# The tail of the last expert and the output of an encoder block, rearranged

## The chip, the cores and the metric

One core of one Trainium2 chip. The metric is the device time of one execution in microseconds; for several runs it is their median.

## The reference, cut to what matters

One layer of a transformer encoder over 512 tokens of width 1024 in float32: two attentions and a gated output projection, then a mixture of 16 experts in which each expert picks its 64 best tokens, and a last RMSNorm.

```python
def expert_choice_ffn(h, w_router, w_gate, w_up, w_down):
    ...
    gate, idx = lax.top_k(jnp.swapaxes(aff, 1, 2), cap)        # 16 experts x 64 tokens
    xe = h[bidx, idx]
    hid = (jax.nn.silu(jnp.einsum('becd,edf->becf', xe, w_gate))
           * jnp.einsum('becd,edf->becf', xe, w_up))
    ye = jnp.einsum('becf,efd->becd', hid, w_down) * gate[..., None].astype(h.dtype)
    return jnp.zeros_like(h).at[bidx, idx].add(ye)
...
    x = x + gt2 * expert_choice_ffn(h2, ...)                    # gt2: 1024 numbers from the condition
return rmsnorm(x, g_final)
```

Each expert has 2048 hidden columns, so its three weights are 8.4 MB each, 403 MB for all experts.

## The kernel before, in words

The first half of the kernel is the attention part. The second half, from about 915 us on, is the loop over experts (L1170). An expert's weights come in twelve pieces of 2.1 MB (n = 0 to 11): gate and up in turn for n < 8, then w_down in four quarters of 512 rows. `weights` (L1032) takes the next of nine ring slots of 16 KB a partition (`wslot`, L1024) and issues the load on SP's queue; SP waits until the slot's last reader is done. A piece gives each partition 16 KB in one run.

For an expert, PE makes the gate and up sums in the PSUM tiles `pg` and `pu` (L1197, two banks each), ACT and DVE make `hid` of them (L1216, L1217), PE transposes it and ACT copies it to `hT` (L1224, L1225). The w_down product (L1232) sums into the bank `py`: 64 rows for the tokens, and the two halves of the 1024 columns on partitions 0 to 63 and 64 to 127. A float32 product is two instructions in the trace, and two products of 64 columns of weights run beside each other on the two halves of the array. DVE scales the result by the gate `gv` and by `gt2` (L1238); ACT rounds to `ye`, DVE takes the remainder (L1242, L1243), so that rounded part and remainder lie on opposite halves of the partitions. The scatter product with the selection matrix `se` (L1166) adds both in one product, into one of the two banks `tpb`, and DVE adds it to `x1` (L1168). PSUM has eight banks, all named: py, px, two tpb, two pg, two pu.

The last expert (e = 15) is different. Its w_down comes in column groups, in the order of `LAST` (L1030): columns 0 to 511 in four loads of 1.05 MB (runs of 2 KB), then 512 to 767 and 768 to 1023 in four loads of 0.52 MB each (runs of 1 KB), so twelve loads in four slots. For each group (L1249) PE sums the product in `py` (L1259): here the two halves of the partitions hold even and odd parts of the sum over the same columns, which the scatter product adds up.

```python
for f in range(4 * ng):
    gg, r = g0 + f // 4, f % 4
    r_ = slice(64 * (r % 2), 64 * (r % 2) + 64)
    T.matmul(py[r_], hT[:, gg, r], w_[:, f], start=gg == 0 and r < 2, stop=gg == 3 and r >= 2)
```

DVE scales (L1261) with `gtf`, which is gt2 for all columns on both halves and was put together by four POOL copies earlier (L1180), ACT and DVE make rounded part and remainder (L1263, L1264), now as two products of 128 rows. For each of the four token groups j follow two products into a `tpb` bank (L1268), the addition (L1269), the square and its sum on ACT (L1270) and the multiplication by g_final on POOL (L1271). After the last group of columns each j has a reduction, an inverse root of its own by twelve small DVE instructions (L1275, L1276 and `rsqrt_mean`, L138 to L152), and the scaling, 512 columns on DVE and 512 on ACT (L1277, L1278). After each second j four output transfers are issued on SP (L1281), each from 32 partitions, 8 KB a partition.

A scheduler places each engine's instructions in an order of its own that respects the dependences; within a queue they then run in order. A PSUM name with one buffer can be taken again once every reader of the tile before is done.

Of the kernel before, what the change touches and what calls it, by code (L numbers as in the profile page):

```python
# [19 lines left out]
P = 128  # L20
# [81 lines left out]
def tile_block(ctx, tc, x, c, positions, w_ada, b_ada, g_norm_mix, w_in, g_q_lat, g_kv_lat, w_uq, w_ukv,  # L102
# [51 lines left out]
    with ExitStack() as pa:  # L154
# [874 lines left out]
        LAST = [(0, 512, g0, 1) for g0 in range(4)] + [(c0, 256, g0, 2) for c0 in (512, 768) for g0 in (0, 2)]  # L1029

        def weights(e, n):


            w_ = wslot()
# [4 lines left out]
            elif e == E_N - 1:  # L1039
                for m in range(2):  # L1040
                    c0, nc_, g0, ng = LAST[2 * (n - 8) + m]
                    for g in range(ng):
                        SP.dma_start(w_[:, 2048 * m + 1024 * g:2048 * m + 2048 // ng * (g + 1)]
                                     .rearrange("p (r d) -> p r d", r=4),
                                     w_down[0, e, 512 * (g0 + g):512 * (g0 + g) + 512, c0:c0 + nc_]
                                     .rearrange("(p r) d -> p r d", p=P))
# [79 lines left out]
    with ExitStack() as pb_:  # L1126
# [43 lines left out]
        for e in range(E_N):  # L1170
            wl = []
            for n in range(12):
                if e == E_N - 1 and n == 4:

                    last = wslot()[:, :2 * D].rearrange("p (a d) -> p a d", a=2)
                    gtf, gfin = last[:, 0], last[:, 1]
# [67 lines left out]


        ssf = wbs.tile([P, NT, 3], F32, name="ssf")
        junk = wbs.tile([P, 2, 512], F32, name="hid", bufs=1)
        wl = [w_[:, 2048 * m:2048 * m + 2048] for w_ in wl[8:] for m in range(2)]
        for g, (c0, n) in enumerate(((0, 512), (512, 256), (768, 256))):  # L1249
            ns = slice(c0, c0 + n)  # L1250
            py = ps.tile([P, 512], F32, name="py", bufs=1)[:, :n]
            for m, (cl, _, g0, ng) in enumerate(LAST):
                if cl != c0:
                    continue
                w_ = wl[m].rearrange("p (f d) -> p f d", f=4 * ng)
                for f in range(4 * ng):
                    gg, r = g0 + f // 4, f % 4
                    r_ = slice(64 * (r % 2), 64 * (r % 2) + 64)
                    T.matmul(py[r_], hT[:, gg, r], w_[:, f], start=gg == 0 and r < 2, stop=gg == 3 and r >= 2)  # L1259
            yf = wbs.tile([P, 512], F32, name="yf", bufs=1)[:, :n]  # L1260
            V.scalar_tensor_tensor(yf, py, gv, gtf[:, ns], op0=OP.mult, op1=OP.mult)  # L1261
            ye = wbs.tile([P, 2, 512], F32R, name="ye", bufs=1)[:, :, :n]
            A.activation(ye[:, 0], yf, AF.Copy)  # L1263
            V.tensor_sub(ye[:, 1], yf, ye[:, 0].bitcast(F32))  # L1264
            for j in range(NT):
                pt = ps.tile([P, 512], F32, name="tpb", bufs=2)[:, :n]
                for a in range(2):
                    T.matmul(pt, se[:, j], ye[:, a], start=a == 0, stop=a == 1)  # L1268
                V.tensor_add(x1[:, j, ns], x1[:, j, ns], pt)  # L1269
                A.activation(junk[:, 0, :n], x1[:, j, ns], AF.Square, accum_out=ssf[:, j, g:g + 1])  # L1270
                G.tensor_tensor(xn[:, j, ns], x1[:, j, ns], gfin[:, ns], op=OP.mult)  # L1271
                if g < 2:
                    continue
# [43 lines left out]
```

## Time and profile before

| What | us |
|---|---|
| runs, median of 3 | 1881.8 |
| runs, lowest and highest | 1881.32, 1885.74 |
| profiled execution, its own time | 1880.84 |
| profiled execution, span from first to last instruction | 1879.06 |

The profile is of one execution. Its busy times are of that span; PE is TensorE's products, PEld its weight loads, DVE VectorE, ACT ScalarE, POOL GpSimd, SP the queue that issues most transfers. PE is busy for 91% of the span and the DMA engines move 283 GB/s on average; both numbers are averages over a first half without a full weight stream and a second half with one.

### The profile page before, as it was taken

The numbers are of one execution on the slowest core, as the hardware profiler recorded it, in microseconds if no ns is written. First come the engines' busy times: TensorE is split into PE (matmuls) and PEld (weight loads), VectorE is DVE, ScalarE is ACT, GpSimd is POOL, SyncE is SP. The second block draws the span as 40 slices with busy tenths as digits, with TensorE's granted clock in tenths as the row PEclk, the third lists the DMA queues.
The fourth block names the chain that finished last, engine by engine and source line by source line (L and its number), as shares of the span: only waits on it lengthen the run. The fifth ranks groups of instructions, "written<-read, shape, count | busy, mean of one in ns | idle before, by whom it ended". The sixth has DMA issues, their size and how long they took to land.

```text
span 1879.1 us, 21596 instructions
## 1 busy us (share of the span) xinstructions
PE 1706.1 (91%) x8876; PEld 1006.4 (54%) x8876; DVE 741.9 (39%) x1393; ACT 391.1 (21%) x768; POOL 156.4 (8%) x148
## 2 busy tenths in 40 slices
PE   3879989999999999999699999999988898889985
PEld 2657667888888888888433333333332333323322
DVE  5877765465564445536612222112122121211213
ACT  3245542222322232223200000000000000000002
POOL 3830000020020001002200000000000000000002
PEclk9999999999999999999899999999999999999998
DMA  9356766534434333231889999999999999999996
GB/s 290 92 150 198 224 187 181 179 122 146 166 112 126 90 90 104 90 90 68 365 336 428 426 427 428 428 427 428 427 427 428 428 428 428 427 428 426 428 424 211
DMA packets 134914, 531.28 MB, mean 283 GB/s; under 512 B 17048, under 2 KB 91288, under 8 KB 108192
## 3 DMA queue, kind: packets, MB, share of 16 engines
q1 hardware_dynamic: 130320, 521.45, 71.8%
q0 software_dynamic: 2080, 6.82, 1.0%
q10 hardware_dynamic: 2416, 1.65, 0.5%
q8 instruction: 70, 1.15, 0.2%
q14 instruction: 28, 0.23, 0.0%
HBM read 520.52 MB, written 16.17 MB: 286 GB/s over the span
## 4 chain that ended last, share of the span: by engine, by line
PE 59%; DMA 26%; DVE 7%; issue 4%; SPq 2%; ACT 1%; POOL 0%; ACTq 0%; DVEq 0%; POOLq 0%
PE pj L452 19%; DMA we<-in_w_gate_dram 14%; PE pu L1197 8%; DMA we<-in_w_up_dram 8%; PE pg L1197 8%; PE pj L866 5%; PE py L1232 4%; PE px L1147 2%; PE sc L608 2%; DVE x L1168 2%; PE sc L937 2%; PE tpb L1166 1%; DMA x<-bkt_d 1%; PE pj L608 1%; DMA cs<-in_consts_dram 1%
## 5 line engine op out<-in xcount | busy, mean ns | idle before, releaser
L452 PE MATMUL pj<-hh,ws 128*128 128x512 f32 x1152 | 373.1, 399 | 1.9 <-DVE ws L428 1.9
L1197 PE MATMUL pg<-we,xT 128*64 128x512 f32 x1024 | 233.4, 595 | 14.3 <-DMA we<-in_w_gate_dram 14.3
L452 PEld LDWEIGHTS pj<-hh,ws 128*128 128x128 f32 x1152 | 217.0, 189 | 53.8 <-DVE ws L428 2.4
L1197 PE MATMUL pu<-we,xT 128*64 128x512 f32 x1024 | 235.0, 595 | 4.8 <-DMA we<-in_w_up_dram 4.8
L1232 PE MATMUL py<-we,hT 128*64 128x512 f32 x960 | 216.6, 597 | 21.3 <-DMA we<-in_w_down_dram 19.4
L452 PE MATMUL pj<-hl,ws 128*128 128x512 f32 x576 | 229.8, 399 | 0.0
L428 DVE TENSOR_TENSOR ws<-raw,ws 128x1024 fp32r<-128x1024 f32 (+2 forms) x108 | 134.0, 1242 | 133.5 <-ACT ws L427 132.7
L427 ACT ACTIVATE ws<-raw 128x1024 fp32r<-128x1024 f32 (+2 forms) x108 | 111.4, 1033 | 251.7 <-PE pj L452 167.9
L1197 PEld LDWEIGHTS pg<-we,xT 128*64 128x64 f32 x1024 | 73.0, 137 | 155.8 <-issue 132.3
L1197 PEld LDWEIGHTS pu<-we,xT 128*64 128x64 f32 x1024 | 72.0, 137 | 146.8 <-issue 133.2
L1232 PEld LDWEIGHTS py<-we,hT 128*64 128x64 f32 x960 | 66.6, 137 | 151.4 <-issue 127.7
L1168 DVE TENSOR_TENSOR x<-x,tpb 128x512 f32<-128x512 f32 x120 | 77.4, 685 | 116.6 <-PE tpb L1166 116.6
L452 PEld LDWEIGHTS pj<-hl,ws 128*128 128x128 f32 x576 | 108.7, 189 | 24.2
L1217 DVE TENSOR_TENSOR hid<-hid,pu 128x512 f32<-128x512 f32 x32 | 20.6, 684 | 219.6 <-PE pu L1197 219.6
L866 PE MATMUL pj<-ws,hh 128*128 128x256 f32 x512 | 94.4, 282 | 0.0
L1216 ACT ACTIVATE hid<-pg 128x512 f32<-128x512 f32 x32 | 17.4, 594 | 298.5 <-PE pg L1197 298.5
L866 PEld LDWEIGHTS pj<-ws,hh 128*128 128x128 f32 x512 | 79.4, 188 | 0.0
L1238 DVE SCALAR_TENSOR_TENSOR yf<-py,gv,gt 128x512 f32<-128x512 f32 x15 | 11.3, 751 | 156.4 <-PE py L1232 156.4
L1180 POOL COPY we<-gt 64x512 f32<-64x512 f32 x4 | 2.4, 610 | 847.3 <-PE pu L1197 847.2
L866 PE MATMUL pj<-ws,hl 128*128 128x256 f32 x256 | 71.6, 280 | 0.0
L1242 ACT ACTIVATE ye<-yf 64x512 fp32r<-64x512 f32 x30 | 18.8, 628 | 253.3 <-DVE yf L1238 253.0
L1147 PE MATMUL px<-xn,gw 128*64 128x512 f32 x256 | 61.6, 613 | 6.0 <-DVE gw L1139 6.0
(368 smaller groups left out, 1985.8 us busy)
## 6 DMA issues: line engine op xcount, KB each, us to landing
we<-in_w_gate_dram SPq DMA_DIRECT2D x64, 2048.0 KB, 7.7
we<-in_w_up_dram SPq DMA_DIRECT2D x64, 2048.0 KB, 35.7
we<-in_w_down_dram SPq DMA_DIRECT2D x60, 2048.0 KB, 39.3
raw<-in_w_in_dram SPq DMA_DIRECT2D x36, 1024.0 KB, 5.3
raw<-in_w_ada_dram SPq DMA_DIRECT2D x19, 1024.0 KB, 5.5
x<-bkt_d SPq DMA_DIRECT2D x104, 128.0 KB, 4.9
raw<-in_w_in_dram SPq DMA_DIRECT2D x16, 512.0 KB, 5.6
stage_d<-stage POOLq DMA_DIRECT2D x26, 256.0 KB, 5.2
```

Source lines behind the costliest of these rows:

```text
L427: A.activation(dst[:, 0], src, AF.Copy)
L428: V.tensor_sub(dst[:, 1], src, dst[:, 0].bitcast(F32))
L452: T.matmul(pu, parts[k // 4][:, a, k % 4, col:col + 128], hx[b][:, k], start=k == 0 and n == 0, stop=k == KD - 1 and n == 2)
L608: T.matmul(out_, w_(a), b_(b), start=i == 0, stop=i == n_ - 1)
L866: T.matmul(pu[:, 256 * j:256 * j + 256], hx[b][:, k, 128 * m:128 * m + 128], parts[k // 4][:, a, k % 4], start=k == 0 and n == 0, stop=k = ...
L937: T.matmul(o, v_, pT_[:, 128 * k:128 * k + 128], start=first, stop=t_ == 3 and k == 3, skip_group_check=True)
L1147: T.matmul(px[64 * dh:64 * dh + 64], gw[:, j, 0], xn[:, j, 512 * dh:512 * dh + 512], start=j == 0, stop=j == NT - 1)
L1168: V.tensor_add(x1[:, j, ds_], x1[:, j, ds_], pt)
L1197: T.matmul(acc[64 * hf:64 * hf + 64, b], xT[:, k], w_[:, r, f0:f0 + 512], start=k == 0, stop=k == KD - 1)
L1217: V.tensor_mul(hid[:, b], hid[:, b], pu[:, b].rearrange("q (p r) -> q r p", r=4))
L1232: T.matmul(py[64 * dh:64 * dh + 64], hT[:, g, r], wd[g][:, r, 512 * dh:512 * dh + 512], start=g == 0 and r == 0, stop=g == 3 and r == 3)
L1242: A.activation(ye[r_, dh], yf[r_], AF.Copy)
```

## The change

The last expert's w_down comes as one whole quarter (rows 0 to 511, one load of 2.1 MB), and its last 1536 rows in columns 0 to 767 (three loads of 1.57 MB, runs of 3 KB) and then 768 to 1023 (three loads of 0.52 MB, runs of 1 KB): seven loads. The product of each column group is made as for the other experts, the first half of the group's columns on partitions 0 to 63 and the second half on 64 to 127, so 384 and then 128 columns an instruction, and the rounding goes by halves as there. `gtf` has that layout now and is loaded by four broadcast transfers on SP. The first group sums in the bank py, its eight scatter products go to eight different banks (px, two tpb, two pg, two pu, py), and the eight additions follow; the second group sums in px, and its eight scatter products go to two tpb banks, added two j at a time. The squares of a whole group go into spare room of the slot `last`. One reduction and one inverse root serve all four j; scaling is 640 columns on DVE and 384 on ACT. The output transfers of partitions 0 to 63 are issued on SP and those of 64 to 127 on ACT, in turn.

```diff
-        LAST = [(0, 512, g0, 1) for g0 in range(4)] + [(c0, 256, g0, 2) for c0 in (512, 768) for g0 in (0, 2)]
+        LAST = ((0, 768), (768, 256))
+        tail_w = []
...
-            elif e == E_N - 1:
-                for m in range(2):
-                    c0, nc_, g0, ng = LAST[2 * (n - 8) + m]
-                    for g in range(ng):
-                        SP.dma_start(...)
+            elif e == E_N - 1 and n == 9:
+                for c0, nc_ in LAST:
+                    for g in range(1, 4):
+                        if c0 == 0:
+                            tail_w.append(w_ if g == 1 else wslot())
+                        SP.dma_start(tail_w[g - 1][:, 4 * c0:4 * c0 + 4 * nc_].rearrange("p (r d) -> p r d", r=4),
+                                     w_down[0, e, 512 * g:512 * g + 512, c0:c0 + nc_].rearrange("(p r) d -> p r d", p=P))
+            elif e == E_N - 1 and n > 9:
+                return tail_w[n - 9]
...
-                    for a in range(2):
+                    for c0, nc_ in LAST:
                         for dh in range(2):
-                            G.tensor_copy(gtf[64 * a:64 * a + 64, 512 * dh:512 * dh + 512], gt2[64 * dh:64 * dh + 64])
+                            a = 5 * D + c0 + nc_ // 2 * dh
+                            SP.dma_start(gtf[64 * dh:64 * dh + 64, c0 // 2:c0 // 2 + nc_ // 2],
+                                         mod_d[a:a + nc_ // 2].unsqueeze(0).to_broadcast([64, nc_ // 2]))
...
+        room = [ps.tile([P, 512], F32, name="tpb", bufs=2), ps.tile([P, 512], F32, name="tpb", bufs=2)]
+        room += [t[:, k] for t in (pg tile, pu tile) for k in range(2)]
+        for i, (c0, n) in enumerate(LAST):
+            m = n // 2
+            hs, ns = slice(c0 // 2, c0 // 2 + m), slice(c0, c0 + n)
+            acc = ps.tile([P, 512], F32, name=("py", "px")[i], bufs=1)[:, :m]
+            for g in range(4):
+                ...
+                        T.matmul(acc[64 * dh:64 * dh + 64], hT[:, g, r], w_[:, r, m * dh:m * dh + m],
+                                 start=g == 0 and r == 0, stop=g == 3 and r == 3)
+            V.scalar_tensor_tensor(yf[:, hs], acc, gv, gtf[:, hs], op0=OP.mult, op1=OP.mult)
+            for dh in range(2):
+                A.activation(ye[r_, dh, hs], yf[r_, hs], AF.Copy)
+                V.tensor_sub(ye[o_, dh, hs], yf[r_, hs], ye[r_, dh, hs].bitcast(F32))
+            if i == 0:
+                room = [ps.tile([P, 512], F32, name="px", bufs=1)] + room + [ps.tile([P, 512], F32, name="py", bufs=1)]
+                for j in range(NT):
+                    for dh in range(2):
+                        T.matmul(room[2 * j + dh][:, :m], se[:, j], ye[:, dh, hs], start=True, stop=True)
+                (eight V.tensor_add to x1)
+            else:
+                for j2 in range(2):
+                    pt = ps.tile([P, 512], F32, name="tpb", bufs=2).rearrange("p (j d) -> p j d", j=2)
+                    (four T.matmul, one V.tensor_add of both j)
             for j in range(NT):
+                A.activation(last[:, 2048:2048 + n], x1[:, j, ns], AF.Square, accum_out=ssf[:, j, i:i + 1])
                 G.tensor_tensor(xn[:, j, ns], x1[:, j, ns], gfin[:, ns], op=OP.mult)
+        V.reduce_sum(ssj, ssf, axis=AX.X)
+        rf = rsqrt_mean(ssj, NT, D, wbs, "rsf")
+        for j in range(NT):
+            V.tensor_scalar(xn[:, j, :640], xn[:, j, :640], rf[:, j:j + 1], None, op0=OP.mult)
+            A.mul(xn[:, j, 640:], xn[:, j, 640:], rf[:, j:j + 1])
+            if j % 2:
+                for c4 in (0, 2, 1, 3):
+                    (SP, A)[c4 // 2].dma_start(out...[c4][:, j - 1:j + 1], xn[32 * c4:32 * c4 + 32, j - 1:j + 1, :])
```

## Rows read from the trace of the kernel before

**Rows 1.** The page: its first line; the rate of the DMA engines in 40 equal slices of the span; and of its list of DMA issues one line (issues, KB each, median us from issue to landing).

```profile
span 1879.1 us, 21596 instructions
GB/s 290 92 150 198 224 187 181 179 122 146 166 112 126 90 90 104 90 90 68 365 336 428 426 427 428 428 427 428 427 427 428 428 428 428 427 428 426 428 424 211
...
we<-in_w_up_dram SPq DMA_DIRECT2D x64, 2048.0 KB, 35.7
```

**Rows 2.** Waits between 1830 and 1882 us: the engine with its instruction, what it waited for, us in all, times, the longest.

```profile
PEld tpb L1268 <- DVE x L1269: 1.4, 3, 0.6
PE py L1259 <- DVE yf L1261: 0.9, 1, 0.9
```

**Rows 3.** The timeline from 1800 to 1882 us, PE, its weight loads and SP's queue: start and length in us, engine, line, operation, count; in brackets the engine's idle time before and what ended it.

```profile
1814.35 0.97 PEld L1209 LDWEIGHTS tpb<-aff,gw 128*128 128x128 f32 x8
...
1834.28 3.65 PE L1197 MATMUL pu<-we,xT 128*64 128x512 f32 x16 [1.28 <-DMA we<-in_w_up_dram]
...
1840.18 7.09 PE L1259 MATMUL py<-we,hT 128*64 128x512 f32 x32
1840.66 0.14 PEld L1259 LDWEIGHTS py<-we,hT 128*64 128x64 f32 x2 [0.29 <-issue]
...
1845.00 0.14 PEld L1259 LDWEIGHTS py<-we,hT 128*64 128x64 f32 x2 [0.34 <-DMA we<-in_w_down_dram]
...
1850.92 1.21 PE L1268 MATMUL tpb<-ye,se 128*128 128x512 f32 x4
...
1854.19 2.81 PE L1259 MATMUL py<-we,hT 128*64 128x256 f32 x24
...
1856.93 0.74 PE L1268 MATMUL tpb<-ye,se 128*128 128x256 f32 x4
...
1857.61 1.08 PE L1259 MATMUL py<-we,hT 128*64 128x256 f32 x8
...
1868.06 6.77 SPq L1281 DMA_DIRECT2D out_dram<-xn  x8
```

**Rows 4.** Busy time in stretches of the last 80 us: the stretch, its length, busy us and instructions of PE, PEld, DVE, ACT and POOL, the granted clock as a share of 2.4 GHz, the busy share of the DMA engines and their GB/s.

```profile
1800.00:1834.20 34.20, 28.64 (x128) 9.64 (x124) 5.49 (x10) 1.67 (x3) 0.00 (x0) 1.00 1.00 419
...
1845.00:1855.00 10.00, 9.09 (x60) 4.63 (x58) 4.38 (x7) 2.77 (x7) 2.25 (x2) 1.00 0.94 304
...
1857.60:1861.00 3.40, 2.53 (x17) 1.59 (x16) 2.69 (x6) 2.34 (x9) 3.18 (x5) 1.00 0.00 0
1861.00:1864.50 3.50, 1.07 (x6) 0.63 (x5) 2.85 (x20) 2.04 (x8) 3.09 (x5) 1.00 0.00 0
1864.50:1868.00 3.50, 0.00 (x0) 0.00 (x0) 3.50 (x40) 1.41 (x3) 0.00 (x0) 0.50 0.00 0
```

**Rows 5.** Instructions by line and shape, from 1840 to 1870 us, the last row from the whole span: busy us, mean ns of one, then idle time before them.

```profile
L1259 PEld LDWEIGHTS py<-we,hT 128*64 128x64 f32 x96 | 6.4, 137 | 8.8 <-issue 4.4 <-DVE yf L1261 1.8 <-ACT hT L1225 0.4
L1271 POOL TENSOR_TENSOR xn<-x,we 128x256 f32<-128x256 f32 x8 | 5.9, 765 | 0.6 <-DVE x L1269 0.4
L1271 POOL TENSOR_TENSOR xn<-x,we 128x512 f32<-128x512 f32 x4 | 5.2, 1342 | 72.3 <-DVE x L1269 72.3
...
L1270 ACT ACTIVATE hid<-x 128x256 f32<-128x256 f32 x8 | 3.3, 415 | 3.1 <-DVE x L1269 2.9
...
L1269 DVE TENSOR_TENSOR x<-x,tpb 128x256 f32<-128x256 f32 x8 | 3.1, 416 | 2.5 <-PE tpb L1268 2.5
L1278 ACT ACTIVATE xn<-xn,rsf_y 128x512 f32<-128x512 f32 x4 | 2.7, 714 | 2.7 <-DVE rsf_t L150 2.7
L1269 DVE TENSOR_TENSOR x<-x,tpb 128x512 f32<-128x512 f32 x4 | 2.6, 684 | 2.5 <-PE tpb L1268 2.4
...
L1277 DVE TENSOR_SCALAR xn<-xn,rsf_y 128x512 f32<-128x512 f32 x4 | 1.9, 481 | 0.1
...
L1261 DVE SCALAR_TENSOR_TENSOR yf<-py,gv,we 128x256 f32<-128x256 f32 x2 | 1.0, 484 | 0.4 <-PE py L1259 0.4
L1263 ACT ACTIVATE ye<-yf 128x256 fp32r<-128x256 f32 x2 | 0.8, 416 | 0.4 <-PE tpb L1268 0.4
L1261 DVE SCALAR_TENSOR_TENSOR yf<-py,gv,we 128x512 f32<-128x512 f32 x1 | 0.8, 751 | 8.0 <-issue 8.0
L1263 ACT ACTIVATE ye<-yf 128x512 fp32r<-128x512 f32 x1 | 0.6, 629 | 7.5 <-DVE yf L1261 7.5
...
L779 PE MATMUL pj<-y,wr 128*32 128x128 f32 x64 | 2.8, 280 | 0.0
```

**Rows 6.** DVE's timeline from 22 to 25 us: the first and the last of the twelve instructions of an inverse root over four columns that runs alone (`rsx`, L141 to L151), in the columns of rows 3.

```profile
22.29 0.17 DVE L141 TENSOR_SCALAR rsx_a<-ss 128x4 f32<-128x4 f32 x1 [3.59 <-ACT ws L382]
...
24.48 0.16 DVE L151 SCALAR_TENSOR_TENSOR rsx_y<-rsx_t,rsx_y 128x4 f32<-128x4 f32 x1
```

**Rows 7.** Single microseconds of the output, in the columns of rows 4.

```profile
1868.00:1869.00 1.00, 0.00 (x0) 0.00 (x0) 0.83 (x3) 1.00 (x3) 0.00 (x0) 0.50 0.37 82
1869.00:1870.00 1.00, 0.00 (x0) 0.00 (x0) 0.00 (x0) 0.26 (x1) 0.00 (x0) 0.50 0.86 180
...
1872.00:1873.00 1.00, 0.00 (x0) 0.00 (x0) 0.00 (x0) 0.00 (x0) 0.00 (x0) 0.50 1.14 270
```

**Rows 8.** The load of x at the start, in the columns of rows 4: four transfers of 32 partitions and 0.52 MB each, two on SP's queue and two on ACT's (L197).

```profile
6.00:9.00 3.00, 2.08 (x10) 2.09 (x10) 2.25 (x17) 0.00 (x0) 0.00 (x0) 1.00 0.96 213
9.00:13.50 4.50, 1.48 (x7) 1.40 (x7) 0.17 (x1) 0.00 (x0) 0.00 (x0) 1.00 0.95 206
```

More of the change, by code (lines that the diff above doesn't have):

```diff
@@ L1026, in wslot @@
             return wb[n].tile([P, 4096], F32, name=f"we{n}")
-        LAST = [(0, 512, g0, 1) for g0 in range(4)] + [(c0, 256, g0, 2) for c0 in (512, 768) for g0 in (0, 2)]
+        LAST = ((0, 768), (768, 256))
+        tail_w = []
         def weights(e, n):
-            w_ = wslot()
+            w_ = None if tail_w else wslot()
             if n < 8:
@@ L1173, in tile_block @@
                 if e == E_N - 1 and n == 4:
-                    last = wslot()[:, :2 * D].rearrange("p (a d) -> p a d", a=2)
-                    gtf, gfin = last[:, 0], last[:, 1]
+                    last = wslot()
+                    gfin, gtf = last[:, :D], last[:, D:D + 512]
                     SP.dma_start(gfin, g_final.unsqueeze(0).to_broadcast([P, D]))
-                    for a in range(2):
+                    for c0, nc_ in LAST:
                         for dh in range(2):
-                            G.tensor_copy(gtf[64 * a:64 * a + 64, 512 * dh:512 * dh + 512], gt2[64 * dh:64 * dh + 64])
+                            a = 5 * D + c0 + nc_ // 2 * dh
+                            SP.dma_start(gtf[64 * dh:64 * dh + 64, c0 // 2:c0 // 2 + nc_ // 2],
+                                         mod_d[a:a + nc_ // 2].unsqueeze(0).to_broadcast([64, nc_ // 2]))
                 wl.append(loaded.pop(0) if loaded else weights(e, n))
@@ L1243, in tile_block @@
                 V.tensor_sub(ye[o_, dh], yf[r_], ye[r_, dh].bitcast(F32))
[L1246 to L1264, printed above, removed]
-            for j in range(NT):
[L1266 to L1270, printed above, removed]
-                G.tensor_tensor(xn[:, j, ns], x1[:, j, ns], gfin[:, ns], op=OP.mult)
-                if g < 2:
-                    continue
-                ssj = wbs.tile([P, 1], F32, name="ssj", bufs=4)
-                V.reduce_sum(ssj, ssf[:, j], axis=AX.X)
-                r = rsqrt_mean(ssj, 1, D, wbs, f"rsf_{j}")
-                V.tensor_scalar(xn[:, j, :512], xn[:, j, :512], r, None, op0=OP.mult)
-                A.mul(xn[:, j, 512:], xn[:, j, 512:], r)
-                if j % 2:
-                    for c4 in range(4):
-                        SP.dma_start(out.rearrange("b (i c q) d -> (b c) i q d", c=4, q=4)[c4][:, j - 1:j + 1],
-                                     xn[32 * c4:32 * c4 + 32, j - 1:j + 1, :])
@@ new lines, in tile_block @@
+        ssj = wbs.tile([P, NT], F32, name="ssj")
+        V.reduce_sum(ssj, ssf, axis=AX.X)
+        rf = rsqrt_mean(ssj, NT, D, wbs, "rsf")
+        for j in range(NT):
+            V.tensor_scalar(xn[:, j, :640], xn[:, j, :640], rf[:, j:j + 1], None, op0=OP.mult)
+            A.mul(xn[:, j, 640:], xn[:, j, 640:], rf[:, j:j + 1])
+            if j % 2:
+                for c4 in (0, 2, 1, 3):
+                    (SP, A)[c4 // 2].dma_start(out.rearrange("b (i c q) d -> (b c) i q d", c=4, q=4)[c4][:, j - 1:j + 1],
+                                               xn[32 * c4:32 * c4 + 32, j - 1:j + 1, :])
```

20 lines of the change are left out of this document (16 added, 4 removed).

## The prediction, made before the changed kernel ran

> **What bounds the kernel now.** I read the page first, then the waits of the last stage, then its timeline row by row, and durations last. The page shows a weight stream: from 990 us on the DMA engines are full at some 428 GB/s, and a w_up load lands 35.7 us after its issue [rows 1]. The last gate and up loads decide when the last expert can go on: PE stands 1.28 us before its last up product, which begins at 1834.28, when that load lands [rows 3]. What follows, 44.8 of the span's 1879.06 us, is what the change touches. In it PE is the bound for 24 us: w_down products from 1840.18, one wait of 0.9 us for DVE to free the one bank py, and the last group of eight at 1857.61 [rows 2, 3]. The w_down loads are never late by more than a hair (0.34 us of idle at 1845.00, where 0.29 is usual). After the last product the chain goes by DVE and ACT to the first output transfer at 1868.06, and 11.0 us of output end the span. So three questions: when is the last product of the expert out, how long is the way from there to the first output transfer, how long does the output take. Now they give 1858.7, 9.4 us and 11.0 us.
>
> **The sum's base.** Its durations come from the profiled execution, 1880.84 us with a span of 1879.06. The median of the runs shown is 1881.8, so I work out a difference and add it to the median. A measurement of this kernel can tell some 0.3% (5.6 us) from no change.
>
> **Edits before the tail.** The four POOL copies into gtf go; POOL had been idle, so nothing is won. Four broadcast loads take their place, 0.26 MB (two of 1536 B, two of 512 B for each of 64 partitions), on SP ahead of eight weight loads. SP issues 35.7 us ahead of need, so their issue costs nothing, but the stream is full: at 428 GB/s they take 0.6 us, at the 304 GB/s of the stretch that ends in 1 KB rows 0.9 [rows 1, 4]. I take 0.7 (sizes between the two): PE restarts at 1835.0 and begins w_down at 1840.9.
>
> **The first 768 columns.** The twelve w_down transfers become seven: 2.1 MB whole, three of 1.57 MB in 3 KB rows, three of 0.52 MB in 1 KB rows. The whole one at 428 GB/s lands at 1835.0 + 4.9 = 1839.9. Row price: 4.19 MB in 2 KB rows took from 1834.28 to 1845.00, 391 GB/s [rows 3]; 3 KB rows lie between that and 428, 4.0 to 3.7 us each, and I take 3.9, nearer the 2 KB row. They land at 1843.8, 1847.7 and 1851.6. PE needs, for each quarter, 16 instructions of 384 columns: 32 of 512 took 7.09 us, 24 of 256 took 2.81, so 0.16 us each, 2.6 a quarter [rows 3]. PE is faster than the stream, waits some 1.3 us twice, and ends at 1851.6 + 2.6 + 0.2 = 1854.4. This is the first new wait: the transfers were covered by PE, now they set its pace.
>
> **The way to the second block.** From rows at 512 and 256 columns [rows 5], at 384: scaling on DVE 0.62, ACT rounding 0.52, DVE remainder 0.55 (as an addition). ACT and DVE do this by halves of the partitions: 0.62 + 0.1 + 0.52 + 0.55 gives the first half at 1856.2, the second 0.6 later. Eight single products follow (four of 512 took 1.21 us, four of 256 0.74, so 0.175 apart [rows 3]): PE is free at 1857.6. A bank for each of them means that none waits for DVE, which was 1.4 us of PE's waiting before [rows 2]. But the second block's sum takes the bank px, which the first product holds, so it waits for that product's addition (0.55 on DVE behind the second remainder at 1856.8: 1857.4, just hidden) and, in PE's queue, stands behind all eight. PE idles 1.8 us here, where the kernel before had the next columns to multiply.
>
> **The second block.** 64 instructions of 128 columns. Streaming alone, half of the 0.107 us at 256 columns, gives 3.4 us. No row has this shape. Weight loads of 128 columns each before a one-column product come at 0.12 us [rows 3], full-width; here two halves load beside each other. With 32-wide weights and 128 columns 64 took 2.8 us, four at a time, 0.175 a step [rows 5]; 32 steps of that are 5.6. If all 64 loads of 137 ns [rows 5] stood in series, 8.8. I take 0.12 a pair, 3.84, near the load row, and 0.2 for the last: out at 1861.65. Its 1.57 MB at 304 GB/s end by 1856.8 and hide. That is 3.0 us later than now.
>
> **To the output.** At 128 columns scaling, rounding and remainders take 0.35 + 0.1 + 0.31 + two of 0.28 and gaps: 1863.05. Products 0.45; two additions of 512 elements, 0.69 and 0.61, end at 1864.8; POOL and ACT start when the first is done. ACT squares four rows of 256 at 0.53 (0.415, and the accumulator's read partly beside it): 1866.5. One reduction 0.2. The inverse root is one chain of twelve instead of four woven together; such a chain, four wide, went from 22.29 to 24.65, 2.35 us [rows 6]: 1869.05. POOL multiplies four rows of 768 (1.92 each by its rows of 512 and 256, from 1857.9) and four of 256 (0.765): 1868.6, hidden by 0.4 us; were the root faster, POOL would be late next. Scaling two rows: DVE 2 x 0.6, ACT 2 x 0.55 beside it: first output at 1870.3, 2.2 us later than now, although the way from the last product shrinks from 9.4 to 8.65.
>
> **The output.** Eight transfers, half on SP, half on ACT. Two issues on ACT stand ahead of its scaling of rows 2 and 3, at 0.85 us each (6.77 for eight on SP [rows 3]); with 1.1 us of scaling the second half of the output is ready 2.8 us after the first, whose data need 3.9, so this hides. The data took 8.4 us now, 250 GB/s, 82 to 270 in single microseconds [rows 7]. Bounds for two queues over opposite halves: 428 GB/s, 4.9 us; or the x load at the start, also 32 partitions a transfer on both queues, 206 to 213 GB/s, 10.0 us [rows 8]. I take 270, the best microsecond of the present output: 7.8 us. The 2.6 us of the 11.0 that are not data stay: 1870.3 + 2.6 + 7.8 = 1880.7.
>
> The Trainium skill's SBUF — State Buffer ("Can I just issue two DMAs to hit both halves?") speaks against this edit: a transfer's own span sets the ports, two at partitions 0 and 64 gained 6%. The trace at the start agrees [rows 8]. By that rule, as an estimate, 213 x 1.06 = 226 GB/s, so 9.3 us of data and 1884.9 in all.
>
> **Sum:** 3.0 at the last product (the 0.7 of gtf among it), less 0.75 on the way to the output, less 0.6 in the output: 1.6 us over 1879.06. Median 1881.8 + 1.6 = **1883.4 us**, inside 0.3%.
>
> **Rivals.**
> **(a) Both halves at full rate.** Data 4.9 instead of 7.8 us: 1880.5. For it: the rate does rise from 180 to 270 GB/s once several transfers are in flight [rows 7]. Against: the x load [rows 8]. Chance 0.23.
> **(b) No gain at all from the second queue**, the x load's rate: 10.0 us, 1885.6. For it [rows 8]; against it the present 250. Chance 0.15.
> **(c) The clock.** The granted clock was 1.0 of 2.4 GHz while PE had 2.53 us of work in 3.4, and fell to 1.2 GHz at 1864.5 after 1.07 us in 3.5 [rows 4]. In the gap from 1854.4 to 1857.6 PE has about 1.4 us of work. If the clock falls there, the second block runs at half speed for part or all of it, at most its 3.84 us more: 1887.2, or 1885.3 where half of it is hit. Against: from 1800 to 1834.2 PE stood for the stream for 5.6 us in all, and the clock kept 1.0 [rows 4]. Chance 0.17.
> **(d) Weight loads in series in the second block,** the rival on the slow side: 64 x 0.137 = 8.8 instead of 3.84 us: 1888.4. It leaves the 0.3% from 0.245 us a pair on (3.84 + 4.0). For it: as many loads as the 256-column blocks had stand before half the columns. Against: two loads ran beside each other in 0.14 us [rows 3]. Chance 0.06.
> **(e) The change doesn't do what it says:** the second sum's bank serializes so that separate banks win nothing. That is in my sum; what is left is that the order on PE puts the second block behind more, under 1 us.
>
> **Chances.** Forecast 0.37, (a) 0.23, (b) 0.15, (c) 0.17, (d) 0.06, 0.02 unseen. Faster by over 0.3% would need (a), free gtf loads, 3 KB rows at 428 and streaming at 0.107 a pair together (1880.5 - 0.7 - 0.6 - 0.4 = 1878.8, still inside) and something unseen: 0.07, 0.05 of it out of (a). Slower by over 0.3%: (d), 0.06, and (b) with (c), 0.06. Same 0.81. The range takes in the bounds of (a) below and of (c) and most of (b) with (c) above: 1878.5 to 1887.5.
>
> **What would show it.** Right: PE's first block ending near 1854.4 behind DMA waits; a PE gap of about 2 us; the last product near 1861.7; a chain of twelve DVE rows near 2.35 us; first output near 1870.3; output windows near 270 GB/s. Wrong: the last product before 1859.5, or output at 400 GB/s (too slow a forecast); a granted clock of 0.5 beside the second block, or pairs over 0.2 us (too fast).

## The result, and the profile after

The changed kernel takes 1891.88 us (median of 6 runs, 1890.28 to 1895.25), the kernel before 1881.56 beside it (6 runs, 1879.92 to 1885.74): ratio 1.0051, 95% interval 1.0039 to 1.0063. It is slower by 10 us, and the forecast of 1883.4 with its range up to 1887.5 missed. The profiled span is 1888.89 us, where the prediction's working led to 1880.7.

The timeline of the changed kernel, in the columns of [rows 3]: PE, and the first output transfers on SP's and ACT's queues.

```profile
1821.65 5.35 PE L1202 MATMUL pg<-we,xT 128*64 128x512 f32 x16 [3.19 <-DMA we<-in_w_gate_dram]
...
1836.35 3.65 PE L1202 MATMUL pu<-we,xT 128*64 128x512 f32 x16 [1.26 <-DMA we<-in_w_up_dram]
...
1842.25 5.74 PE L1264 MATMUL py<-we,hT 128*64 128x384 f32 x32
1850.69 2.80 PE L1264 MATMUL py<-we,hT 128*64 128x384 f32 x16 [2.71 <-DMA we<-in_w_down_dram]
1855.92 4.50 PE L1264 MATMUL py<-we,hT 128*64 128x384 f32 x16 [2.43 <-DMA we<-in_w_down_dram]
1862.34 0.44 PE L1276 MATMUL px<-ye,se 128*128 128x384 f32 x1 [1.92 <-DVE ye L1270]
1865.29 4.38 PE L1264 MATMUL px<-we,hT 128*64 128x128 f32 x64
1879.52 4.13 SPq L1299 DMA_DIRECT2D out_dram<-xn  x4
1879.53 0.39 ACTq L1299 DMA_DIRECT2D out_dram<-xn  x1
```

PE no longer sets the pace: it stands for the third and the fourth load of w_down, and the fourth block, the same 16 instructions as the third, takes 4.50 us in place of 2.80. The first row shows the same a stage earlier: after 3.19 us of waiting, 16 instructions take 5.35 us that otherwise take 3.65 (the row of 1836.35); there the next load is late anyway. The wait for DVE that [rows 2] showed at `py` is gone (PE now stands for DVE behind each block, 1.9 and 2.0 us), and this one stands first among PE's waits from 1842 us on:

```profile
PE py L1264 <- DMA we<-in_w_down_dram: 5.1, 2, 2.7
```

The stretches of the changed kernel, in the columns of [rows 4] (the clock is the third figure from the end, GB/s the last):

```profile
1806.00:1811.00 5.00, 4.35 (x18) 1.44 (x16) 2.57 (x4) 0.00 (x0) 0.00 (x0) 1.00 1.03 354
1811.00:1816.00 5.00, 5.00 (x30) 2.42 (x28) 0.16 (x1) 0.58 (x1) 0.00 (x0) 1.00 1.05 338
...
1857.30:1860.40 3.10, 3.10 (x12) 0.98 (x8) 0.00 (x0) 0.00 (x0) 0.00 (x0) 0.59 0.00 0
1860.40:1865.30 4.90, 2.75 (x12) 2.06 (x10) 4.10 (x8) 2.19 (x5) 1.13 (x1) 0.79 0.01 3
1865.30:1870.00 4.70, 4.37 (x65) 4.13 (x64) 1.83 (x5) 2.60 (x6) 4.70 (x4) 0.85 0.01 2
```

and the first two of them in the kernel before:

```profile
1806.00:1811.00 5.00, 4.34 (x18) 1.44 (x16) 2.40 (x4) 0.00 (x0) 0.00 (x0) 1.00 1.01 426
1811.00:1816.00 5.00, 5.00 (x32) 2.43 (x29) 0.33 (x2) 0.58 (x1) 0.00 (x0) 1.00 1.02 429
```

For ten microseconds the stream ran at 354 and 338 GB/s in place of 426 and 429, with the engines as busy as before: 0.8 MB short. Those are the microseconds in which the four gtf loads are in flight. And the granted clock fell twice at the end: after PE's two waits, and again in the gap behind the first block. The output, in the columns of [rows 7], is the part that got faster:

```profile
1880.00:1881.00 1.00, 0.00 (x0) 0.00 (x0) 0.33 (x1) 0.51 (x2) 0.00 (x0) 0.50 0.75 156
...
1883.00:1884.00 1.00, 0.00 (x0) 0.00 (x0) 0.00 (x0) 0.00 (x0) 0.00 (x0) 0.50 0.97 377
1884.00:1885.00 1.00, 0.00 (x0) 0.00 (x0) 0.00 (x0) 0.00 (x0) 0.00 (x0) 0.50 1.09 410
```

The time before the last expert varies by several us from one execution to another (its first up product begins anywhere from 1802 to 1811 us), so I compare three stretches of each profiled execution: **A**, from the last expert's first up product to its last (in the timeline above 1836.35 is the last one); **B**, from there to the first output transfer; **C**, from there to the end. In the table, e1 to e17 are the experiments told below. The ratio is to runs of the kernel before that were timed beside each (their medians went from 1879.9 to 1881.6 us), so ratios can be compared, and medians only roughly.

| run | A | B | C | median us | ratio to before, 95% |
|---|---|---|---|---|---|
| before | 29.8 | 33.8 | 11.0 | 1881.56 | |
| after | 32.4 | 43.2 | 9.4 | 1891.88 | 1.0051 (1.0039 to 1.0063) |
| e1 order of loads | 32.6 | 38.6 | 9.7 | 1887.11 | 1.0031 (1.0021 to 1.0040) |
| e2 POOL copies | 29.6 | 43.4 | 9.6 | 1887.55 | 1.0033 (1.0020 to 1.0045) |
| e3 own bank | 32.5 | 39.6 | 9.7 | 1887.01 | 1.0031 (1.0019 to 1.0042) |
| e4 before, halves | 29.6 | 33.8 | 9.6 | 1878.24 | 0.9989 (0.9979 to 0.9999) |
| e5 two wide loads | 32.2 | 41.7 | 9.5 | 1889.39 | 1.0048 (1.0033 to 1.0064) |
| e6 three mends | 29.6 | 38.0 | 9.9 | 1885.02 | 1.0023 (1.0013 to 1.0034) |
| e7 and POOL relieved | 29.6 | 35.9 | 9.5 | 1881.51 | 1.0009 (0.9999 to 1.0019) |
| e8 before, halves, one root | 29.6 | 33.8 | 9.6 | 1879.57 | 0.9994 (0.9984 to 1.0004) |
| e9 separate rows | 32.3 | 43.4 | 9.4 | 1892.69 | 1.0062 (1.0049 to 1.0075) |
| e10 other row | 32.4 | 43.1 | 9.7 | 1889.60 | 1.0055 (1.0042 to 1.0069) |
| e11 fill, too much | 32.7 | 53.9 | 9.6 | 1903.83 | 1.0131 (1.0118 to 1.0145) |
| e12 output on SP | 32.3 | 43.3 | 11.0 | 1893.03 | 1.0073 (1.0061 to 1.0085) |
| e13 fill | 32.3 | 42.1 | 9.8 | 1889.71 | 1.0049 (1.0038 to 1.0061) |
| e14 4 KB packets | 31.0 | 43.4 | 9.6 | 1890.80 | 1.0045 (1.0033 to 1.0058) |
| e15 three blocks | 30.9 | 36.0 | 9.7 | 1882.66 | 1.0009 (0.9999 to 1.0019) |
| e16 three blocks, late squares | 30.6 | 34.6 | 9.7 | 1882.12 | 0.9998 (0.9986 to 1.0011) |
| e17 e4 again | 29.6 | 33.8 | 9.6 | 1879.89 | 0.9986 (0.9975 to 0.9998) |

After against before: A +2.6, B +9.4, C -1.6, 10.4 in all, as the medians say. In column A the nine executions with the short gtf loads have 32.2 to 32.7, and those with POOL copies 29.6 to 29.8, but for e15 and e16. In these two the stream ran at its full rate (421 to 437 GB/s from 1819 to 1831 us in e15), yet one up load came late (PE waited for it 2.58 and 2.38 us), and the 16 instructions behind it took 5.35 us in place of 3.65; why it came late is open.

### The profile page after: what moved, and what is told of

The parts are those of the page before. It is cut to its first block, busy times and chain, and to the rows that moved or that the text cites. A ratio compares the mean times of both kernels' runs of the same rounds, so it can differ in the third digit from the quotient of the medians.

```text
span 1888.9 us, 21575 instructions
## 1 busy us (share of the span) xinstructions
PE 1707.5 (90%) x8900; PEld 1007.4 (53%) x8900; DVE 741.2 (39%) x1352; ACT 390.5 (21%) x761; POOL 153.7 (8%) x140
## 4 chain that ended last, share of the span: by engine, by line
PE 59%; DMA 29%; DVE 7%; SPq 2%; issue 1%; ACT 1%; POOL 0%; DVEq 0%; ACTq 0%; POOLq 0%
PE pj L452 19%; DMA we<-in_w_gate_dram 13%; PE pu L1202 7%; PE pg L1202 7%; DMA we<-in_w_up_dram 5%; PE pj L866 5%; PE py L1237 4%; DMA we<-in_w_down_dram 3%; DMA x<-bkt_d 2%; PE sc L608 2%; DMA we<-in_g_final_dram 2%; PE pj L608 2%; PE px L1150 2%; DVE x L1171 2%; PE sc L937 2%; PE tpb L1169 1%
## 5 line engine op out<-in xcount | busy, mean ns | idle before, releaser
L1290 POOL TENSOR_TENSOR xn<-x,we 128x768 f32<-128x768 f32 (+1 forms) x8 | 10.0, 1292 | 935.6 <-DVE x L1280 933.8
```

## The experiments

### The scale row: where A's 2.6 us come from

**e2.** The loads undone, by POOL copies into the new layout.

```
-for c0, nc_ in LAST: (four SP.dma_start into gtf)
+for dh, at, h, c, n_ in (...five pieces...):
+    G.tensor_copy(gtf[64*dh:64*dh+64, at:at+n_], gt2[64*h:64*h+64, c:c+n_])
```

> The changed kernel, with gtf put together by five POOL copies instead of four broadcast loads on SP. Theory (the narrow loads slow the whole stream beyond their bytes, 2.5 us in all): the last up product begins near 1834.2 instead of 1836.35, the span is 1886.9 or a little less. Rival 1 (only their bytes cost, 0.7 us): last up product near 1835.6. Rival 2 (the shift comes from the run, not from the loads): 1836.3 as it is.

A is 29.6 again: the loads cost 2.8 us, while B stays 43.4. **e5** loads the same bytes by two transfers over 128 partitions.

> The changed kernel, with the scale row for gtf loaded by two transfers over all 128 partitions (one for 768 columns, one for 256) in place of four over 64 partitions each; the 0.26 MB written stay the same. From the first to the last up product of the last expert the kernel before took 29.8 us, the changed one 32.4, and 29.6 with POOL copies in place of the loads. Theory, that the number or the narrow shape of the four transfers holds the full-width stream up: about 30.4 us (29.6 and 0.6 to 0.7 of bytes), a time near 1889.9 us. Rival, that the broadcast itself (128 short rows from one place in DRAM) is what costs: again 32.0 to 32.5 us, time near 1891.9.

A stays 32.2: neither the number of four nor the 64 partitions is it. (Its B is 41.7 for another reason, told with the clock.) **e9** and **e10** leave the shape and change the source: `w_up[0, 0, 64*dh:64*dh+64, ...]`, 64 separate rows, and `g_final[...]`, another repeated row.

> The changed kernel with its four gtf transfers as they are in shape and size, but read from 64 separate rows of w_up in place of one row repeated (the values in gtf are then not the right ones). From the first to the last up product of the last expert the changed kernel takes 32.4 us, with POOL copies 29.6. If reading one place of DRAM 64 times is what slows the 2 MB loads beside it: about 30.3 us. If short packets as such do it, or their writes: 32 us or more. Time near 1889.5 or 1891.9.

> The changed kernel with its four gtf transfers repeating parts of g_final's row in place of the row in mod_d (the values in gtf are then not the right ones). If it matters that the repeated row lies in a tensor that the kernel itself wrote: 30.3 us from the first to the last up product of the last expert. If a repeated short row as such does it: 32 to 32.5 us again, and the time of the changed kernel, 1891.9.

Both stay above 32: no repeated row, and no tensor that the kernel wrote itself. **e14** doubles the bytes and makes the packets 4 KB.

```
-four SP.dma_start(gtf[64*dh:64*dh+64, ...], mod_d[...].to_broadcast([64, nc_ // 2]))
+SP.dma_start(gtf, mod_d[5*D:6*D].unsqueeze(0).to_broadcast([P, D]))
```

> The changed kernel with gtf loaded whole, one transfer of 4 KB for each of 128 partitions (0.52 MB, twice the bytes) in place of four of 1.5 KB and 0.5 KB for 64; scaling reads the half that it needs, in two DVE instructions of 64 partitions. If short packets slow the 2 MB loads in flight beside them: 29.6 us of POOL copies and 1.2 of bytes, 30.8 us from the first to the last up product of the last expert in place of 32.4, and the time near 1890.9 (0.6 us lost to the split scaling). If it is any second small transfer beside that of g_final that does it: over 32 us, 1892.5.

A is 31.0, where bytes alone make 30.8. The same two stretches as above, of e9 and then of e14:

```profile
1806.00:1811.00 5.00, 4.36 (x20) 1.56 (x18) 2.57 (x4) 0.00 (x0) 0.00 (x0) 1.00 1.00 332
1811.00:1816.00 5.00, 5.00 (x32) 2.44 (x30) 0.16 (x1) 0.58 (x1) 0.00 (x0) 1.00 1.02 334
```

```profile
1806.00:1811.00 5.00, 4.36 (x18) 1.39 (x14) 1.68 (x4) 0.00 (x0) 0.00 (x0) 1.00 1.01 424
1811.00:1816.00 5.00, 5.00 (x29) 2.32 (x28) 0.95 (x2) 0.51 (x1) 0.00 (x0) 1.00 1.02 425
```

With packets of 1.5 KB and 0.5 KB the stream drops to 332, with 4 KB it doesn't. The runs don't separate the size of the packets from their number (256 against 128). In the records of single packets the small ones take little themselves (34 to 51 ns for 0.5 KB, 65 to 84 for 1.5 KB); the 16 KB packets of the weights in flight beside them take 720 to 860 ns in place of 613 (medians over 2 us each, in the changed kernel and e9). Why, no run here shows.

### The order of the loads, and the clock

The diff's loops name three loads of 1.57 MB and then three of 0.52 MB. The scheduler's order on SP is another: large and small in turn. The issues from 1817 to 1819 us of the changed kernel (count, KB each), when two large ones are still to come:

```profile
we<-in_w_down_dram SPq DMA_DIRECT2D x1, 1536.0 KB
we<-in_w_down_dram SPq DMA_DIRECT2D x1, 512.0 KB
```

**e1** holds the small ones behind the large ones.

```
+with tc.issue_after(nc.cur_bb.bb.instructions[-1]) if c0 else ExitStack():
     SP.dma_start(tail_w[g - 1][...], w_down[...])
```

> The changed kernel, with the three loads of 1 KB rows held behind the three of 3 KB rows on SP's queue. Theory (order of the loads): two 1 KB loads of 1.4 to 1.5 us each stood ahead of the last 3 KB load, which landed at 1855.9; now it lands 2.9 us earlier, near 1853.0, and the first block ends 2.9 to 4.7 us earlier than 1860.4 (the more, the less of it runs at 1.2 GHz): span 1884.2 to 1886.0 instead of 1888.9. Rival (the order is hidden, since the second block needs the 1 KB loads anyway and its start is set by the scatter and the bank px): span within 1 us of 1888.9.

B falls by 4.6 us. PE in e1:

```profile
1849.91 2.80 PE L1265 MATMUL py<-we,hT 128*64 128x384 f32 x16 [1.20 <-DMA we<-in_w_down_dram]
1853.72 2.80 PE L1265 MATMUL py<-we,hT 128*64 128x384 f32 x16 [1.00 <-DMA we<-in_w_down_dram]
...
1860.50 3.71 PE L1265 MATMUL px<-we,hT 128*64 128x128 f32 x64
```

The blocks are 3.81 us apart in place of 5.23: a 1.57 MB load is worth 3.8, the 0.52 MB load that stood between them 1.4. Two such stand before the fourth block, 2.8 us. The waits are short now, the block takes 2.80, and the second block 3.71 in place of 4.38. All of the 4.6 us are won up to the end of the first block, 24.12 to 19.48 us after the last up product; from there to the first output it is 19.06 and 19.08. So is the rest of the 4.6, 1.7 us, the clock? **e11** filled PE's waits with products that nobody reads.

```
+if i == 0 and g > 1:
+    for r in range(14):
+        T.matmul(room[0][:64, :384], hT[:, 0, r % 4], wd[0][:, r % 4, :384], start=True, stop=True)
```

> The changed kernel with 28 more products of 384 columns into a bank that nobody reads, queued on PE among the w_down products so that PE stands idle less while it waits for the third and fourth loads (14 of 0.175 us are 2.45 us, about one wait). Theory, that the idle wait lets the clock fall and that this costs 1.7 us at the fourth load's block: the granted clock stays 1.0 there, the block takes 2.80 us in place of 4.50, the first block ends 1.7 us earlier after the last up product (22.4 us in place of 24.1), time near 1890.2. Rival, that the clock has another cause or the added products delay the block: 24 us or more, time 1892 or more.

This was mis-sized: a product is two instructions, and on one half of the partitions each takes 0.33 us (17 took 5.65), so they delayed the blocks by 10 us; the clock stayed 1.0, which decides nothing. **e13** has six, in pairs over both halves, behind each of two loads.

> The changed kernel with 12 more products of 384 columns in pairs over both halves, six behind the second load's block and six behind the third's, into a bank that nobody reads. By the earlier run a product is two instructions and an instruction costs 0.325 us alone, so 0.175 in a pair: six are 2.1 us, less than either wait (2.71 and 2.43 us). Theory, that the idle wait lets the clock fall and that this costs 1.7 us: granted clock 1.0 to 1860, the fourth block 2.80 us in place of 4.50, the first block ends 22.4 us after the last up product in place of 24.1, time near 1890.2. Rival, that the clock falls for another reason: 24 us again, 1892.

PE in e13, and its clock from 1856 to 1860 us:

```profile
1850.74 2.80 PE L1270 MATMUL py<-we,hT 128*64 128x384 f32 x16 [0.76 <-DMA we<-in_w_down_dram]
1853.35 2.13 PE L1265 MATMUL tpb<-we,hT 128*64 128x384 f32 x12
1855.94 2.80 PE L1270 MATMUL py<-we,hT 128*64 128x384 f32 x16 [0.46 <-DMA we<-in_w_down_dram]
...
1862.49 3.71 PE L1270 MATMUL px<-we,hT 128*64 128x128 f32 x64
```

```profile
1856.00:1860.00 4.00, 2.74 (x16) 1.00 (x16) 0.62 (x1) 0.50 (x1) 0.00 (x0) 1.00 0.04 14
```

The fourth block starts where it did (1855.94, it was 1855.92) and takes 2.80: the clock fell because PE stood idle, and at that block cost 1.7 us. e5 shows the same from the other side. There the granted clock fell one block earlier (0.56 from 1849 to 1852 us), the wait for the fourth load took up the loss (0.80 in place of 2.43), and B is 1.5 shorter than in the changed kernel; its third and fourth block:

```profile
1848.79 4.50 PE L1263 MATMUL py<-we,hT 128*64 128x384 f32 x16 [2.71 <-DMA we<-in_w_down_dram]
1854.08 2.80 PE L1263 MATMUL py<-we,hT 128*64 128x384 f32 x16 [0.80 <-DMA we<-in_w_down_dram]
```

From the first block's end to the second's last product e13 saved 1.8 more (1858.79 to 1866.20, it was 1860.46 to 1869.67). But in e13 B fell by only 1.1, and the time by less than can be told: what was gained at PE was lost behind it. Where, the second block's two remainders on DVE and POOL's first four multiplications show, in the changed kernel, e1 and e13:

```profile
1864.17 7.26 POOL L1290 TENSOR_TENSOR xn<-x,we 128x768 f32<-128x768 f32 x4 [933.77 <-DVE x L1280]
1870.45 1.45 DVE L1270 TENSOR_TENSOR ye<-yf,ye 64x128 fp32r<-64x128 f32 x2 [0.38 <-ACT ye L1269]
```

```profile
1860.26 7.25 POOL L1291 TENSOR_TENSOR xn<-x,we 128x768 f32<-128x768 f32 x4 [929.60 <-DVE x L1281]
1864.99 2.67 DVE L1271 TENSOR_TENSOR ye<-yf,ye 64x128 fp32r<-64x128 f32 x2 [0.38 <-ACT ye L1270]
```

```profile
1862.84 7.21 POOL L1296 TENSOR_TENSOR xn<-x,we 128x768 f32<-128x768 f32 x4 [933.53 <-DVE x L1286]
1866.97 3.54 DVE L1276 TENSOR_TENSOR ye<-yf,ye 64x128 fp32r<-64x128 f32 x2 [0.38 <-ACT ye L1275]
```

A remainder takes 0.29 us alone. The earlier the pair starts, the longer it takes: in all three it ends 0.15 to 0.47 us after POOL's four multiplications. So the second fall of the clock, in the gap behind the first block, cost nothing here: with it or without it, the first output came 19.06 (the changed kernel), 19.08 (e1) and 19.62 us (e13) after the first block's end.

### Behind the last product

**e3** gives the second block's sum a bank that no product holds.

```
-room = [px] + room + [py]
+room = room + [py, None]
+    if 2 * j + dh == 7: (add room[0] first; the eighth product takes its bank)
```

> The changed kernel, with the second block's sum in px by itself; the eight scatter products of the first block take py and the other six banks, and the eighth waits for the first tpb. Theory (the shared bank px puts the second block behind scaling, rounding, products and one addition): its 4.4 us of products go into PE's waits for loads and for DVE, first output some 5 us earlier, span near 1884. PE then stands less and the granted clock may stay up, 1 to 2 us more. Rival (the chain over DVE and ACT after the first block sets the end): under 2 us, span above 1887.

The second block's products now fill PE's waits for the loads, the last weight product ends at 1858.5 in place of 1869.7 (23.2 us after the last up product in place of 33.3), the clock holds without any filling up to there, and B still falls by only 3.5, between the theory and the rival. POOL and the start of the inverse root in e3:

```profile
1862.37 9.90 POOL L1294 TENSOR_TENSOR xn<-x,we 128x768 f32<-128x768 f32 x8 [933.22 <-DVE x L1284]
...
1868.52 1.05 DVE L141 TENSOR_SCALAR rsf_a<-ssj 128x4 f32<-128x4 f32 x1
1869.60 0.65 DVE L143 TENSOR_SCALAR rsf_g<-rsf_a 128x4 int32<-128x4 int32 x1
...
1872.32 0.16 DVE L151 SCALAR_TENSOR_TENSOR rsf_y<-rsf_t,rsf_y 128x4 f32<-128x4 f32 x1
```

An instruction of four columns takes 0.64 to 1.05 us until POOL is done at 1872.27, and 0.16 from then on. **e6** joins the mends of e1, e2 and e3.

> The changed kernel with the three mends together: POOL copies for gtf, 1 KB loads behind the 3 KB ones, a bank of its own for the second block's sum. If the gains add up (2.8 us for the copies, 2.9 us for the order, on top of the run with its own bank, whose first output stood at 1874.9): last weight product near 1853, first output near 1869.2, end of span near 1878.8, time near 1881.5, no difference from the kernel before. POOL's eight multiplications are then the bound, and the first instructions of the root take 0.65 us each beside them. Rival, that clock or DVE take the gains back as they did when only the order was mended: first output after 1871, time over 1883.5.

```profile
1863.18 9.96 POOL L1293 TENSOR_TENSOR xn<-x,we 128x768 f32<-128x768 f32 x8 [78.93 <-DVE x L1283]
1869.77 3.40 DVE L141 TENSOR_SCALAR rsf_a<-ssj 128x4 f32<-128x4 f32 x1
```

Here one such instruction of DVE stands 3.40 us, to POOL's end at 1873.14. The Trainium skill (SBUF — State Buffer, "SBUF: two separate sides") says that GpSimd and DVE instructions of some kinds, those with two inputs in SBUF among them, share a port pair as a lock that one instruction holds to its end. These rows agree. So do DVE's additions, which read one operand from PSUM: they take 0.55 us beside POOL as without it (at 1866.30 and 1862.90 us of the changed kernel). But 3.40 is longer than any one multiplication of POOL there (on average 1.84 for 768 columns, 0.73 for 256). The gains don't add up: B is 38.0, where e1's 4.6 and e3's 3.5 would make it 35.1. **e7** takes half of POOL's multiplications out of the way, those of the last 256 columns.

```
+if i == 0: (POOL multiplies the 768-column block alone)
+V.scalar_tensor_tensor(xn[:, j, 768:], x1[:, j, 768:], rf[:, j:j+1], gfin[:, 768:], op0=mult, op1=mult)
```

> As the run with three mends, and POOL multiplies the first 768 columns alone: for the last 256 the factor g_final goes into the last scaling on DVE (one instruction of three operands for 256 columns, a plain one for 256, ACT takes 512). Theory, that POOL and the DVE instructions slowed beside it are the bound after the last product: the root runs at 0.16 us an instruction, first output near 1866.6, end near 1876, time near 1878.7, about 3 us under the run with three mends. Rival, that ACT's eight squares are the bound and POOL stands in nobody's way: under 1 us of gain, time near 1881.

B falls by 2.1 more, to 35.9, and the kernel is level with the one before. The root starts now when ACT's squares are done (DVE waits 1.87 us for them), and its first row still takes 0.70 beside POOL. The last 2 us: **e15** splits 512, 256 and 256 columns.

> The run with three mends and POOL relieved, with the last w_down in blocks of 512, 256 and 256 columns as in the kernel before (loads in the order of the blocks, scatter products by halves of the partitions, one inverse root, output on two queues). Loads by their rows: 4.9, three of 2.7, six of 1.43, so the last lands 21.6 us after the last up product begins, last weight product 22.8 after it; 256 columns of additions and squares are left then, not 1024, so about 9.2 us to the first output as in the kernel before and 9.5 of output. Theory, that too much DVE and ACT work stands behind the late end of a 768-column block: first output 32.0 us after the last up product (35.9 with two blocks, 33.8 in the kernel before), time near 1878.0, about 3.5 under two blocks. Rival, that 1 KB rows and more steps take it back: 34 us or more, time over 1880.

36.0, the rival's side. Two waits in its trace, ACT's last rounding behind squares (what it rounds was ready at 1859.56) and the second pair of products behind DVE:

```profile
1860.82 0.62 ACT L1268 ACTIVATE ye<-yf 64x128 fp32r<-64x128 f32 x2
...
1864.11 1.11 PE L1275 MATMUL pg<-ye,se 128*128 128x128 f32 x4 [0.78 <-DVE x L1276]
```

**e16** takes them away but for some 0.5 us at the rounding (banks `tpb` for the last block, each block's squares queued behind the next one's rounding).

> The run with three blocks, its last block's scatter products in the two banks named tpb (in that run both pairs took halves of one tile, and the second pair stood 0.78 us behind DVE's addition of the first), and ACT's squares of each block queued behind the next block's rounding (there the last rounding stood 1.2 us behind squares). Theory, that these two waits make the way from the last weight product to the output 12.2 us: it falls to 10.0 us, the first output stands 33.8 us after the last up product as in the kernel before, time near 1880. Rival, that the way is bound by ACT's and DVE's own work: 12 us again, time 1882.7.

B is 34.6, 0.8 longer than in the kernel before, but the way from the last product to the output is 12.0 us still, as the rival had it: it is bound by ACT's and DVE's own work. POOL has 0.9 us of it: DVE's remainder of 128 columns, 0.29 us alone, takes 0.77 and 0.69 beside POOL.

```profile
1862.19 0.77 DVE L1269 TENSOR_TENSOR ye<-yf,ye 64x128 fp32r<-64x128 f32 x1 [0.20 <-ACT ye L1268]
...
1863.71 0.69 DVE L1269 TENSOR_TENSOR ye<-yf,ye 64x128 fp32r<-64x128 f32 x1
```

### The output and the root

**e4** puts the output alone on the two queues, in the kernel before; **e17** is the same kernel timed again; **e12** undoes it in the changed kernel; **e8** is e4 with one inverse root.

```
-for c4 in range(4): SP.dma_start(...)
+for c4 in (0, 2, 1, 3): (SP, A)[c4 // 2].dma_start(...)
```

> The kernel before, with the output transfers alone changed: partitions 0 to 63 on SP, 64 to 127 on ACT, in turn. Theory (two queues over opposite halves move the output faster: 8.3 us from first issue to last landing instead of 10.0): span 1877.4 instead of 1879.06, 1.7 us under the kernel before. Rival (the gain in the changed kernel is that all four rows are ready within 2 us of each other): output near 10 us, same time as before.

> The kernel before with its output on two queues, timed a second time beside it, since the first interval (0.9979 to 0.9999) only just left 1. If the split is a gain: 9.6 us from the first output transfer to the end in place of 11.0, ratio 0.9990 or 0.9995, upper end at most 1.0003. If not: 1.0000 or more.

> The changed kernel with its eight output transfers all on SP's queue, as in the kernel before. In the kernel before the split took 1.4 us off the time from the first output transfer to the end (11.0 to 9.6). If the split is worth that here too: 10.8 to 11.0 us from the first output transfer to the end in place of 9.4, time near 1893.4. Rival, that the split gains nothing once all four rows are scaled at about the same time: 9.4 to 9.8 us, time 1891.9.

> The kernel before with two parts of the change: output by halves of the partitions on two queues, and one inverse root over four columns in place of four roots. The halves alone gave 1878.24 us (first output to end 9.6 us in place of 11.0). Theory, that the four woven roots (48 DVE rows of 0.14 and their scalings between) set the first output at 1868.1: the reduction at 1864.0, a root of 2.4 us, scaling 1.2, so first output 1867.5 and a time near 1877.6. Rival, that POOL's last multiplication (to 1864.5) slows the first instructions of the single root as it does in the changed kernel: first output near 1868.1, time as with the halves alone, 1878.2.

The split is worth 1.4 us in the kernel before and 1.6 in the changed one. The issues in e4, and then in e12:

```profile
1867.95 4.08 SPq L1281 DMA_DIRECT2D out_dram<-xn  x4
1867.95 0.86 ACTq L1281 DMA_DIRECT2D out_dram<-xn  x2
1869.67 2.40 ACTq L1281 DMA_DIRECT2D out_dram<-xn  x2
```

```profile
1880.19 6.90 SPq L1299 DMA_DIRECT2D out_dram<-xn  x8
```

The last issue in e4 ends at 1872.1, in the kernel before at 1874.8 [rows 3]. One queue can hardly feed more than it did: eight issues of 0.26 MB in 6.77 us [rows 3] and 6.90 us (e12) make 310 and 304 GB/s, an estimate, and its best microsecond has 270 [rows 7] and 303 (e12). So the split may win by its issues alone; whether it matters that the queues serve opposite halves of the partitions, no run here separates. In both timings the interval ends below 1: e4 is the version that beats both kernels, by 0.11% and 0.14%. One root brings nothing (B 33.8 with it and without it): in e8 its chain starts at 1862.49, but its first row takes 0.44 us beside POOL, and all rows wait for it.

## Why the prediction was wrong

The sum went from 1880.7 to 1888.9 in the span. By the prediction's own steps:

- **"I take 0.7" for the gtf loads: failed.** Measured 2.6 to 2.8 (A; e2). Bytes were costed, and what short packets do to the transfers beside them was not. Of the error, 1.9 us.
- **"They land at 1843.8, 1847.7 and 1851.6": failed, the largest error.** The price of a 1.57 MB load, 3.9, was right (3.8 in e1), the order was not: the loop's order was taken for the queue's. From the last up product to the first block's end 19.4 us were forecast; e1, with the loop's order, takes 19.48, the changed kernel 24.12. Of these 4.7 us 2.8 are two small loads that come first (e1), and the rest the clock (1.7 at the fourth block, e13).
- **Rival (c) named the clock, at the wrong place.** The fall that hurt came in the DMA waits, which rows with shorter waits had been held to exclude. In the gap that the rival named it fell too, and that cost nothing that shows (e1).
- **"Two of 0.28" for the second block's remainders: failed.** From the first block's end to the end of these remainders 8.65 us were forecast (1854.4 to 1863.05), and 11.4 measured; 11.1 in e1 and 11.7 in e13, where the clock held. By the prediction's own rows they lie beside POOL's multiplications of 768 columns (1857.9 to 1865.6); it asked whether POOL would be late, and not what POOL does to DVE. With the root, 2.6 in place of 2.35, its first row 0.43 beside POOL, the way from the first block's end to the first output is 19.1 us in place of 15.9: 3.2 of the error. That POOL holds DVE up is read from the traces; no run takes POOL away altogether.
- **The second block on PE.** The way to it took 4.83 in place of 3.2: some 1 us is the clock (3.93 in e1, 3.70 in e13), the rest the second product's wait for the second half's remainder, which the forecast had at 1856.8 and then let no product wait for. Its products were right: 3.84 forecast, 3.71 at the full clock, 4.38 as it fell. Rival (d), loads in series, did not occur. None of this reached the output, as e1 shows, since the remainders waited for POOL anyway.
- **The output** went 1.0 us better: 9.4 in place of 10.4, between the forecast and rival (a). The Trainium skill's rule on two transfers (SBUF — State Buffer, "Can I just issue two DMAs to hit both halves?"), by which it would have been 1884.9, is not what the stores here show: 377 and 410 GB/s in single microseconds, against a best of 270 [rows 7] and 303 (e12) from one queue.

The terms: 1.9 + 4.7 + 3.2 - 1.0 = 8.8, less 0.5 by which the last expert began earlier in this execution: 8.2 with unrounded terms, the whole difference. The prediction saw that the loads would set PE's pace. What it had wrong is their order and price, and what stands behind them: the mends of the stream came through (e2 in A, e1 in B), but most of the time won at PE was given back at DVE beside POOL, and at ACT (e3, e6, e13).

What stays open: why packets of 0.5 and 1.5 KB slow 16 KB packets beside them, why an up load came late in e15 and e16, whether the output gains by the second queue or by the halves, and how far the way behind the last product could be cut with POOL out of DVE's way altogether, which wasn't tried.

## What to carry to other kernels

Read the order of loads from the queue, not from the loop, and cost a small load by its packets and by what is in flight beside it, not by its bytes. Where loads set PE's pace, look for work to put in its waits (e3): behind waits of 2.7 and 2.4 us a block took 1.7 more. When a chain of short DVE instructions ends the path, see whether POOL is at work beside it: time won ahead of such a chain can be lost in it (e13).

## What the runs showed of the hardware that was not expected

- 0.26 MB in packets of 1.5 and 0.5 KB took 10 us of the stream from 427 to some 345 GB/s; 0.52 MB in 4 KB packets left it at 424 (e14).
- Stores from opposite halves of the partitions on two queues reach 410 GB/s in the best microsecond, on one queue 270 and 303; loads into quarters at the start, on the same two queues, had 206 to 213 [rows 8].
- A DVE instruction on four columns took 0.16 us alone, 0.64 to 1.05 and once 3.40 beside POOL's multiplications (e3, e6); DVE's additions from PSUM took 0.55 with and without POOL beside them.
- An instruction of a product on one half of the partitions took 0.33 us for 384 columns, in pairs over both halves 0.175 (e11, e13).
